# Bias of a residual added from SBUF, rows stored plainly, sums in two passes, nine warm-up matmuls

## The chip, the cores and the metric

The kernel runs on one core of one Trainium2 chip. The metric is device microseconds of one execution, and of several runs the median counts. A profiled execution gives, beside its own device time, the span from its first to its last instruction.

## The reference

The reference is a decoder trunk of two layers on 1024 tokens of 1024 channels, in float32. Layer 0 mixes tokens with a causal Conformer convolution of 31 taps, layer 1 with sliding-window attention. What matters here is what both layers do around the mixer's output `y`:

```python
x = layer_norm(DEEPNORM_ALPHA * x + y, mix_ln_g[i], mix_ln_b[i])
x = layer_norm(DEEPNORM_ALPHA * x + sq_relu_mlp(x, mlp_w_up[i], mlp_w_down[i]),
               mlp_ln_g[i], mlp_ln_b[i])
x = x + (p[i] @ ple_w_proj[i]) * jax.nn.sigmoid(x @ ple_w_gate[i])
```

The normed `x` of the first line is used twice in the second: as input of the MLP, and, times ALPHA, as the residual that is added to the MLP's output. With `xhat` for the normed rows before gain and bias, this residual is ALPHA * g * xhat + ALPHA * b, with `g = mix_ln_g[i]` and `b = mix_ln_b[i]`. The second term is the same for every token; it is the bias of which the title speaks.

## The kernel before

**How the program is made.** The code records all instructions with their reads and writes (`Recorder`, L224) and then orders them by a planner (`schedule`, L343): it plays the program on estimated durations (`cost`) and landing times (`LANDING`, L100), takes on each engine the ready instruction with the lowest priority number, and so fixes the order of every engine's queue and of the DMA queue of SP. `with nc.later(n)` moves the priority of what it encloses n places back, and `with nc.after(op)` lets the planner start it only when `op` has ended in its own play; on the chip only the data and the order of the queues bind. So a change in one place can move instructions elsewhere. All instructions are issued from one helper line (L493 in the profile), so groups are told by their tiles.

**Precision.** Each operand of a product is split into a high and a low part (`split`, L578: ACT casts the high one, DVE subtracts to get the low one), and each product is three matmuls. Weights come by SP into `raw` and are split into `wh` and `wl`, five buffers of each. Large products use Winograd's seven half-size products for eight, for which sums and differences of operands are made on DVE.

**The start (`conv`).** `warm_up` (L843) issues WARM = 7 matmuls on zeros while the first inputs load. Then, in 40 steps, come the input product of the convolution by blocks of 128 channels (`conv_in`, later `conv_seven`), the taps as matmuls on shifted copies (`taps`), whose weights go through `bo`, `E` and `B` buffers, and the stores of intermediate results. At step BIASED = 3 the two layers' bias rows are loaded into the `bo` buffers, multiplied by ALPHA on POOL, and written as one row each to DRAM (`bias0`, `bias1`); in the eight steps after that, `bias_rows` (L746) fills the 1024 rows of the DRAM tensor `mid` of layer 0 with that row, two DMAs of 256 KB (from DRAM to DRAM, on SP's queue) for each of eight tiles of 128 tokens. The same is done for layer 1 in the last down group of layer 0.

**From the convolution to the MLP.** `conv_ln` (L1103) norms the convolution's result in two halves of tokens, each of eight channel blocks. The result is read back from DRAM (`reload`): the first half into X buffers, the second into A buffers. The second half's reads are planned after block SECOND = 4 of the first half, and the reads of the input rows x (into B buffers, four tiles of tokens) after block XB = 3. `mix_out` multiplies by the output weights. `mix_norm` (L707) makes `xhat` for a tile of tokens; its last tiles call `column_forms` (L755), which turns pairs of tiles into channel-major form on PE, applies gain and bias on ACT, and splits the result into the operands of the MLP. Of the four pairs, the first two are kept as they are; with the last two, token sums for Winograd's products T[1] to T[4] are made on DVE, each split as soon as it is there, channel block by channel block. T[4] lives in B buffers.

**The residual.** `keep_row` (L738) multiplies xhat by ALPHA * g in place and adds it to `mid` by an accumulating DMA on POOL's queue: at once for the rows in B buffers, and one by one during the up product for those in A (`late_rows`). Thirty-two such DMAs of 256 KB run in all, sixteen for each layer.

**The down product.** It goes in three groups of chunks, DOWN = (0, 1, 2), (3, 4), (5, 6, 7) (`down_seven`, L1569). A group runs seven products, each of 24 matmuls for every chunk, and adds each to one or two quarters of x in SBUF (`add_to`); operands are made in eight blocks of `xTh` and `xTl`, two for each chunk of a product. In the first group (`begin`), `residual` (L1631) adds `mid` to x: sixteen accumulating DMAs on POOL's queue, four after the second, fifth, sixth and seventh product. The middle group also prepares gate weights (`gate_plain`). The last group norms the rows (`layer_norm`), and `ple_seven` adds the gated embedding.

Of the kernel before, what the change touches and what calls it, by code (L numbers as in the profile page):

```python
# [10 lines left out]
F32 = mybir.dt.float32  # L11
F32R = mybir.dt.float32r
AF = mybir.ActivationFunctionType
ALU = mybir.AluOpType
AXIS = mybir.AxisListType.X

P = 128
T = 1024
D = 1024
KB = D // P  # L20
NT = T // P
HT = 512
# [5 lines left out]
ALPHA = 4.0 ** 0.25  # L28
# [18 lines left out]
BEHIND = 200  # L47
ROWS_BY = 0
BIAS_BY = 200
BIASED = 3  # L50
XB, SECOND = 3, 4
FIRST_OUT = "shifted", 6, 1, 1
PLAIN = 2
ZC = 288
# [19 lines left out]
XHAT = ['av'] * 8  # L74
ROWS_LATE = 400, 400, 400, 400
COLUMN_SLACK = 1500
RAWS = "raw", "zz", "raw", "raw"
MIX = (0, ((0, 1, 4, 5),)), (1, ((0, 1), (4, 5), (2, 3), (6, 7))), (0, ((2, 3), (6, 7)))
TAIL = (0, (2,)), (1, (0, 2)), (0, (3,)), (1, (1, 3))
# [2 lines left out]
DOWN = (0, 1, 2), (3, 4), (5, 6, 7)  # L82
SUMMED = (0, 7)
GRAIN = 64
WARM = 7
EARLY = 2
URGENT = 200
PLAN = (
# [439 lines left out]
class Emit:  # L528
# [209 lines left out]
    def keep_row(self, i, t, q, g):  # L738

        nc = self.nc  # L740
        v = self.x[t][q]
        cols = slice(q * HT, (q + 1) * HT)
        nc.vector.scalar_tensor_tensor(out=v, in0=v, scalar=ALPHA, in1=g, op0=ALU.mult, op1=ALU.mult)
        nc.gpsimd.dma_start(self.mid[i][t][:, cols], v, accum_op=ALU.add)

    def bias_rows(self, i, tiles=range(NT)):  # L746

        for t in tiles:
            for q in range(2):
                cols = slice(q * HT, (q + 1) * HT)  # L750
                at = np.broadcast_to(np.arange(cols.start, cols.stop), (P, HT))
                src = View(self.bias[i].buf, at, P, (("fn", lambda a, cols=cols: a[:, cols].to_broadcast([P, HT])),))
                self.nc.sync.dma_start(self.mid[i][t][:, cols], src)

    def column_forms(self, i, p):  # L755

        nc = self.nc
        tt, sub = nc.vector.tensor_tensor, ALU.subtract
        if p == 0:
            self.cols = {}  # L760
            self.T = {}
        for k in range(4):
            ps = self.ps("tr")
            nc.slack = COLUMN_SLACK
            for q in range(2):
                for j in range(2):
                    o = q * 256 + j * P
                    nc.tensor.transpose(ps[:, o : o + P], self.x[2 * p + j][q][:, k * P : (k + 1) * P], self.ident)
            nc.slack = 0.0
            v = self.column_home(k, p) if p < 2 else self.sb("z")  # L770
            for q in range(2):
                kb = k + 4 * q
                c = slice(q * 256, (q + 1) * 256)
                gc, bc = (self.mixc[:, 16 * i + 8 * m + kb : 16 * i + 8 * m + kb + 1] for m in range(2))
                nc.scalar.activation(v[:, c], ps[:, c], AF.Identity, bias=bc, scale=gc)
            at = slice(p * 256, (p + 1) * 256)
            if p < 2:
                self.cols[k, p] = v
                w = v.rearrange("p (q t) -> p q t", q=2)
                self.split(w, *[x[:, k : k + 5 : 4, at] for x in (self.xTh, self.xTl)])  # L780
                continue
            r = self.cols[k, p - 2]
            L, R = slice(0, 256), slice(256, HT)
            to = slice(p % 2 * 256, (p % 2 + 1) * 256)
            T = {n: [x[:, to] for x in self.token_home(n, k)] for n in range(1, 5)}
            s = self.sb("z")[:, L]
            tt(out=v[:, L], in0=v[:, L], in1=r[:, L], op=sub)
            tt(out=s, in0=v[:, R], in1=v[:, L], op=sub)
            self.split(s, *T[2])
            tt(out=r[:, L], in0=s, in1=r[:, L], op=sub)  # L790
            self.split(r[:, L], *T[3])
            self.split(v[:, L], *T[1])
            self.split(v[:, R], *[x[:, k + 4, at] for x in (self.xTh, self.xTl)])
            tt(out=r[:, R], in0=r[:, R], in1=s, op=sub)
            self.split(r[:, R], *T[4])

    def column_home(self, k, p):

# [44 lines left out]
    def warm_up(self):  # L843
# [4 lines left out]
        ps = self.ps()  # L848
        for k in range(WARM):
            nc.tensor.matmul(ps, z[:, 0:P], z, start=True, stop=True)  # L850
# [29 lines left out]
    def conv(self):  # L880

        nc, d, ws = self.nc, self.d, self.ws
# [188 lines left out]
        def reload(c, e):  # L1071

            Z[c, e] = self.sb("XA"[e])
            src = View(zd[c].buf, np.arange(T), P, (("fn", lambda a: a[:, e * HT : (e + 1) * HT]),))
            nc.sync.dma_start(Z[c, e], src)
# [54 lines left out]
        last = None  # L1130
        zd = [nc.tile(f"zd{c}", (P, T), F32, "DRAM") for c in range(8)]
# [6 lines left out]
        for n in range(32 + LAG):  # L1138
            next(ins, None)
            if n == ready:  # L1140
                for k in range(4):
                    self.differences(k)
            if n in (ready, ready + 1):
                for j in ((3, 2), (4, 1))[n - ready]:
                    for k in range(4):
                        self.split_form(j, k)
            if n == BIASED:
                for i in range(2):
                    for q, v in enumerate(self.load_row("bo", d["mix_b"][i : i + 1])):
                        nc.gpsimd.tensor_scalar(out=v, in0=v, scalar1=ALPHA, scalar2=0.0, op0=ALU.mult, op1=ALU.add)  # L1150
                        nc.sync.dma_start(self.bias[i][:, q * HT : (q + 1) * HT], v[0:1])
            if BIASED < n <= BIASED + NT:
                self.bias_rows(0, (n - BIASED - 1,))
            if n >= LAG:
                next(outs, None)
            if n == BACK[0]:
                for c in range(BACK[1]):
                    reload(c, 0)
            if n == 30 + LAG:
                last = nc.ops[-1]  # L1160
            if n >= 32 + LAG - 8 // EARLY * EMBEDDED:
                with nc.later(EMBED_BY):
                    for k in range(min(EARLY, 8 * EMBEDDED - HELD - made)):
                        next(early)
                        made += 1
# [4 lines left out]
        with nc.after(marks["shifted", 7, 1, 1]):  # L1170
            bo = self.load_row("bo", d["b_out"])
# [11 lines left out]
        r = conv_stats()  # L1183
# [58 lines left out]
    def mix_out(self, i, w, g, gate):  # L1242
# [3 lines left out]
        for n, (cc, groups) in enumerate(MIX):  # L1246
            g_ = gate[n > 0]
            ws.add(*[lambda ap=w[cc, u], tag=RAWS[u], g_=g_: self.prep(ap, gate=g_, tag=tag) for u in range(4)])
        for cc, groups in MIX:
# [319 lines left out]
    def down_seven(self, i, cs, begin, end):  # L1569

        nc, d = self.nc, self.d
# [36 lines left out]
        def product(ops, to, bank=None, last=False):  # L1608
            new = bank is None
            bank = [self.ps() for t in range(4)] if new else bank  # L1610
            if last and to == [(0, 1)]:
                for k in range(3):
                    nc.move("ps", "tr")
            every = [(k, t) for k in range(len(ops)) for t in range(4)]
            for k, t in sorted(every, key=lambda x: x[::-1]) if last else every:
                self.part(bank[t], *ops[k], t, new and k == 0, k == len(ops) - 1, not new)
            for t in range(4):
                for h, q in to:
                    self.add_to(t + 4 * h, q, bank[t])
            with nc.after(nc.ops[-1]):  # L1620
                for k in range(0 if begin or end else min(2, len(plain))):
                    self.gate_plain(i, *plain.pop(0))
            for t in range(4 if last and not i else 0):
                with nc.after(bank[t]):
                    self.bias_rows(1, (t + 4 * to[0][0],))
            for t in range(4 if last else 0):
                with nc.later(LATE + NORM_STEP * t if to == [(0, 1)] else 0):
                    self.layer_norm(t + 4 * to[0][0], gb)
            return bank

        def residual(h, q):  # L1631
            for t in range(4 * h, 4 * h + 4) if begin else ():
                nc.gpsimd.dma_start(self.x[t][q], self.mid[i][t][:, q * HT : (q + 1) * HT], accum_op=ALU.add)

        def each(f, own=False):
            return [formed(*f(c), own) for c in order]
# [281 lines left out]
    def attention(self):  # L1918
# [95 lines left out]
        for cc, n in TAIL[1:]:  # L2014
            ws.add(*[lambda ap=d["w_o"][cc, u], tag=RAWS[u]: self.prep(ap, tag=tag) for u in range(4)])
        for k, (cc, pairs) in enumerate(TAIL):
# [94 lines left out]
    def program(self):  # L2111
        nc = self.nc
# [12 lines left out]
        for i in range(2):  # L2125
            for t in range(NT):
                nc.slots(f"mid{i}_{t}", [f"mid{i}_{t}"])
            for c in range(NC):
                for k in range(8):
                    nc.slots(f"hid{i}_{c}_{k}", [f"hid{i}_{c}_{k}"])  # L2130
        for k in ("qd", "kd", "ad", "bias0", "bias1", *[f"zd{c}" for c in range(8)]):
            nc.slots(k, [k])
        self.bias = [nc.tile(f"bias{i}", (1, D), F32, "DRAM") for i in range(2)]
        self.qd = nc.tile("qd", (NH * P, T), F32, "DRAM")
        self.kd = nc.tile("kd", (4 * P, 2 * T), F32, "DRAM")
        self.ad = nc.tile("ad", (P, 4 * T), F32, "DRAM")
# [141 lines left out]
```

## Time and profile before

| | us |
|---|---|
| median of three runs | 2102.75 (2100.43 to 2102.86) |
| profiled execution | 2099.18 |
| its span | 2097.5 |
| PE busy in it | 2078.6 |
| DVE, ACT, POOL busy | 1598.6, 1145.6, 205.5 |

The profile's page gives busy times, the chain of work that ended last, and groups of instructions. A timeline row is start, length, engine, line, operation, output<-inputs, shapes and count, and in brackets the idle time of the engine before it with what ended it. A row of the windows view has, for a stretch, the busy time of PE, PE's weight loads, DVE, ACT and POOL with their numbers of instructions, then the granted clock of PE, the share of the 16 DMA engines in use, and GB/s. In the waits view a row is who waited for whom: us in total, times, longest. Matmuls overlap, so the time that one takes of PE is the distance between starts, not its length. Stages by time: convolution to 290, output product and preparation of the MLP to 400, up product of layer 0 to 670, down product to 960, gate and embedding to 1100, attention to 1340, then layer 1 in the same order.

### The profile page before, as it was taken

What the parts mean: (1) busy time and instruction counts of PE and PEld (TensorE: products, weight loads), DVE (VectorE), ACT (ScalarE), POOL (GpSimd) and SP (SyncE); (2) the same over time, 40 slices, a digit from 0 to 9 for tenths busy, and PEclk for the clock granted to TensorE, in tenths of its full rate; (3) what the DMA queues carried; (4) which work ended last, traced back from release to release, by engine and by line L of the source; (5) the groups of instructions that cost most, each with busy time, mean ns of one, the idle gap of its engine ahead of it and who ended that gap; (6) DMA issues with size and microseconds to landing.
All of it is one profiled execution on the core that took longest, in us unless ns stands there. A gap on an engine that the chain in (4) does not pass through costs nothing.

```text
span 2097.5 us, 28728 instructions
## 1 busy us (share of the span) xinstructions
PE 2078.6 (99%) x9863; PEld 1731.5 (83%) x9863; DVE 1598.6 (76%) x2502; ACT 1145.6 (55%) x2086; POOL 205.5 (10%) x365
## 2 busy tenths in 40 slices
PE   9999999999999999999999999999999999999998
PEld 7888878888888888888889878878888888888887
DVE  7777798877775768779774798886777656788796
ACT  6566765755555544424433798675555555344343
POOL 0000001000000010000000576110000000100000
PEclk9999999999999999999999999999999999999999
DMA  8878955488868878555777672556888697885526
GB/s 254 264 218 244 323 186 134 145 250 273 266 235 289 253 202 279 186 181 141 244 217 219 214 238 85 141 171 192 255 257 274 205 328 220 222 284 169 163 75 197
DMA packets 232858, 455.70 MB, mean 217 GB/s; under 512 B 22148, under 2 KB 79748, under 8 KB 232712
## 3 DMA queue, kind: packets, MB, share of 16 engines
q1 hardware_dynamic: 223352, 436.83, 63.7%
q0 software_dynamic: 9216, 16.78, 5.1%
q8 instruction: 77, 1.26, 0.3%
q14 instruction: 69, 0.57, 0.1%
q10 hardware_dynamic: 144, 0.26, 0.1%
HBM read 313.27 MB, written 148.91 MB: 220 GB/s over the span
## 4 chain that ended last, share of the span: by engine, by line
PE 88%; DVE 6%; DMA 2%; ACT 2%; issue 1%; POOL 1%; SPq 0%; DVEq 0%; ACTq 0%; POOLq 0%
PE ps L493 67%; PE tr L493 20%; DVE wl L493 1%; DVE A L493 1%; DMA mid<-bias 1%; DVE B L493 1%; ACT z L493 1%; DVE xTl L493 1%; DVE sm L493 1%; DMA raw<-in_w_in_dram 1%; DMA mid<-B 1%; DVE X L493 0%; DVE z L493 0%; ACT t L493 0%; POOL sm L493 0%
## 5 line engine op out<-in xcount | busy, mean ns | idle before, releaser
L493 PE MATMUL ps<-xTh,wh 128*128 128x512 f32 (+1 forms) x672 | 261.9, 391 | 1.2 <-ACT xTh L493 1.2
L493 PE MATMUL ps<-xTl,wh 128*128 128x512 f32 (+1 forms) x672 | 262.4, 391 | 0.2 <-DVE xTl L493 0.2
L493 PE MATMUL ps<-xTh,wl 128*128 128x512 f32 (+1 forms) x672 | 261.8, 390 | 0.3 <-DVE wl L493 0.3
L493 DVE TENSOR_TENSOR wl<-raw,wh 128x1024 fp32r<-128x1024 f32 (+2 forms) x146 | 153.1, 1049 | 101.3 <-ACT wh L493 100.9
L493 PE MATMUL ps<-xTh 128*128 128x512 f32 x552 | 214.7, 389 | 0.0
L493 PE MATMUL ps<-xTl,xTh 128*128 128x512 f32 x552 | 214.7, 389 | 0.0
L493 PE MATMUL ps<-xTh,xTl 128*128 128x512 f32 x552 | 214.7, 389 | 0.0
L493 ACT CAST wh<-raw 128x1024 fp32r<-128x1024 f32 (+2 forms) x146 | 132.0, 906 | 98.4 <-PE ps L493 67.2
L493 ACT CAST wh<-g 128x512 fp32r<-128x512 f32 x152 | 90.0, 620 | 154.5 <-PE ps L493 59.3
L493 ACT CAST xTh<-wh 128x1024 fp32r<-128x1024 f32 x84 | 88.3, 1051 | 152.9 <-PE ps L493 119.1
L493 DVE TENSOR_TENSOR wl<-g,wh 128x512 fp32r<-128x512 f32 x152 | 101.5, 686 | 64.0 <-ACT wh L493 63.3
L493 PE MATMUL ps<-wl,xTh 128*128 128x512 f32 (+1 forms) x400 | 150.1, 376 | 0.0
L493 PE MATMUL ps<-wh,xTh 128*128 128x512 f32 (+1 forms) x400 | 150.0, 376 | 0.0
L493 PE MATMUL ps<-wh,xTl 128*128 128x512 f32 (+1 forms) x400 | 149.4, 375 | 0.2 <-DVE xTl L493 0.2
L493 PEld LDWEIGHTS ps<-xTh,wh 128*128 128x128 f32 x672 | 126.5, 189 | 27.7 <-ACT xTh L493 1.9
L493 PEld LDWEIGHTS ps<-xTh,wl 128*128 128x128 f32 x672 | 126.7, 189 | 26.1 <-DVE wl L493 0.7
L493 PEld LDWEIGHTS ps<-xTl,wh 128*128 128x128 f32 x672 | 126.9, 189 | 24.9 <-DVE xTl L493 0.9
L493 DVE TENSOR_TENSOR xTl<-wh,xTh 128x1024 fp32r<-128x1024 f32 x84 | 102.6, 1221 | 56.8 <-ACT xTh L493 56.6
L493 PEld LDWEIGHTS ps<-xTl,xTh 128*128 128x128 f32 x552 | 103.6, 188 | 21.7
L493 PEld LDWEIGHTS ps<-xTh 128*128 128x128 f32 x552 | 103.6, 188 | 21.5
L493 PEld LDWEIGHTS ps<-xTh,xTl 128*128 128x128 f32 x552 | 103.6, 188 | 21.3
L493 DVE TENSOR_TENSOR xTl<-wl,xTh 128x1024 fp32r<-128x1024 f32 x76 | 92.4, 1218 | 1.7 <-ACT xTh L493 1.7
(398 smaller groups left out, 5056.1 us busy)
## 6 DMA issues: line engine op xcount, KB each, us to landing
wh<-hid SPq DMA_DIRECT2D x84, 512.0 KB, 4.5
raw<-in_w_up_dram SPq DMA_DIRECT2D x67, 512.0 KB, 4.7
wl<-in_w_down_dram SPq DMA_DIRECT2D x58, 512.0 KB, 4.7
hid<-t SPq DMA_DIRECT2D x92, 256.0 KB, 3.6
hid<-zz SPq DMA_DIRECT2D x68, 256.0 KB, 4.3
raw<-hid SPq DMA_DIRECT2D x26, 512.0 KB, 4.2
mid<-bias SPq DMA_DIRECT2D x32, 256.0 KB, 6.8
z<-scr SPq DMA_DIRECT2D x32, 256.0 KB, 4.7
```

Of the source, the lines that this page charges most:

```text
L493: getattr(getattr(nc, o.eng), o.name)(*a, **k)
```

## The change

- `warm_up` issues nine matmuls on zeros for seven.
- The gates of `conv`'s end: x rows after block 1 of the first half (XB), the second half's reads after block 6 (SECOND).
- `bias_rows`, its 32 fills, the DRAM rows and the step that made them are gone.
- `keep_row` stores its row plainly on SP's queue.
- In the middle down group the bias row is loaded into the two `bo` buffers and multiplied by ALPHA on POOL, and `residual` adds it to x by accumulating DMAs from SBUF on POOL's queue, at the same places of the group as in the first one.
- `column_forms` makes the sums of a channel block first; the splits of T[3], T[1], the plain quarter and T[4] get priorities 40, 60, 60 and 60 places later (FORMED), so that they come in a second pass.

```diff
-BIASED = 3
-XB, SECOND = 3, 4
+XB, SECOND = 1, 6
+FORMED = 40, 60, 60, 60
-WARM = 7
+WARM = 9
 def keep_row(self, i, t, q, g):
     ...
     nc.vector.scalar_tensor_tensor(out=v, in0=v, scalar=ALPHA, in1=g, op0=ALU.mult, op1=ALU.mult)
-    nc.gpsimd.dma_start(self.mid[i][t][:, cols], v, accum_op=ALU.add)
-
-def bias_rows(self, i, tiles=range(NT)):
-    ...
+    nc.sync.dma_start(self.mid[i][t][:, cols], v)
 def column_forms(self, i, p):
     ...
     self.split(s, *T[2])
     tt(out=r[:, L], in0=s, in1=r[:, L], op=sub)
-    self.split(r[:, L], *T[3])
-    self.split(v[:, L], *T[1])
-    self.split(v[:, R], *[x[:, k + 4, at] for x in (self.xTh, self.xTl)])
     tt(out=r[:, R], in0=r[:, R], in1=s, op=sub)
-    self.split(r[:, R], *T[4])
+    for n, (a, to) in enumerate((
+        (r[:, L], T[3]), (v[:, L], T[1]), (v[:, R], [x[:, k + 4, at] for x in (self.xTh, self.xTl)]), (r[:, R], T[4])
+    )):
+        with nc.later(FORMED[n]):
+            self.split(a, *to)
 def conv(self):
     ...
-            if n == BIASED:
-                for i in range(2):
-                    for q, v in enumerate(self.load_row("bo", d["mix_b"][i : i + 1])):
-                        nc.gpsimd.tensor_scalar(out=v, in0=v, scalar1=ALPHA, scalar2=0.0, op0=ALU.mult, op1=ALU.add)
-                        nc.sync.dma_start(self.bias[i][:, q * HT : (q + 1) * HT], v[0:1])
-            if BIASED < n <= BIASED + NT:
-                self.bias_rows(0, (n - BIASED - 1,))
 def down_seven(self, i, cs, begin, end):
     ...
-            for t in range(4 if last and not i else 0):
-                with nc.after(bank[t]):
-                    self.bias_rows(1, (t + 4 * to[0][0],))
+        if not begin and not end:
+            bias = self.load_row("bo", d["mix_b"][i : i + 1])
+            for v in bias:
+                nc.gpsimd.tensor_scalar(out=v, in0=v, scalar1=ALPHA, scalar2=0.0, op0=ALU.mult, op1=ALU.add)
+
         def residual(h, q):
-            for t in range(4 * h, 4 * h + 4) if begin else ():
-                nc.gpsimd.dma_start(self.x[t][q], self.mid[i][t][:, q * HT : (q + 1) * HT], accum_op=ALU.add)
+            for t in range(4 * h, 4 * h + 4) if not end else ():
+                src = self.mid[i][t][:, q * HT : (q + 1) * HT] if begin else bias[q]
+                nc.gpsimd.dma_start(self.x[t][q], src, accum_op=ALU.add)
```

More of the change, by code (lines that the diff above doesn't have):

```diff
@@ L743, in keep_row @@
         nc.vector.scalar_tensor_tensor(out=v, in0=v, scalar=ALPHA, in1=g, op0=ALU.mult, op1=ALU.mult)
-        nc.gpsimd.dma_start(self.mid[i][t][:, cols], v, accum_op=ALU.add)
-    def bias_rows(self, i, tiles=range(NT)):
[L748 to L753, printed above, removed]
+        nc.sync.dma_start(self.mid[i][t][:, cols], v)
     def column_forms(self, i, p):
@@ L2130, in program @@
                     nc.slots(f"hid{i}_{c}_{k}", [f"hid{i}_{c}_{k}"])
-        for k in ("qd", "kd", "ad", "bias0", "bias1", *[f"zd{c}" for c in range(8)]):
+        for k in ("qd", "kd", "ad", *[f"zd{c}" for c in range(8)]):
             nc.slots(k, [k])
-        self.bias = [nc.tile(f"bias{i}", (1, D), F32, "DRAM") for i in range(2)]
         self.qd = nc.tile("qd", (NH * P, T), F32, "DRAM")
```

## The prediction

> **What bounds the kernel now.** I read the page first, then windows of the span, then the matmuls that waited, then the chain back from those waits. The page says that TensorE is the bound nearly throughout:
>
> ```profile
> span 2097.5 us, 28728 instructions
> PE 2078.6 (99%) x9863; PEld 1731.5 (83%) x9863; DVE 1598.6 (76%) x2502; ACT 1145.6 (55%) x2086; POOL 205.5 (10%) x365
> ```
>
> The change removes no matmul and adds two, so nothing can be won except in the 18.9 us in which PE is idle and where its clock is low. The timeline of PE alone shows where; the bracket is idle time before the row and who ended it. The rows without a bracket are there for the spacing of matmuls.
>
> ```profile
> 1.51 3.35 PE L493 MATMUL ps<-t 128*128 128x512 f32 x7 [1.51 <-DVE t L493]
> 6.02 1.22 PE L493 MATMUL ps<-xTh,wh 128*128 128x512 f32 x2 [1.15 <-ACT xTh L493]
> 9.60 0.63 PE L493 MATMUL ps<-xTh,wl 128*128 128x512 f32 x1
> 10.03 0.63 PE L493 MATMUL ps<-xTh,wh 128*128 128x512 f32 x1
> 10.46 0.44 PE L493 MATMUL ps<-xTl,wh 128*128 128x512 f32 x1
> 11.43 0.40 PE L493 MATMUL ps<-xTh,wl 128*128 128x512 f32 x1
> 11.66 0.39 PE L493 MATMUL ps<-xTh,wh 128*128 128x512 f32 x1
> ...
> 65.68 2.29 PE L493 MATMUL ps<-z,E 128*128 128x256 f32 x9 [3.98 <-DVE E L493]
> 290.90 0.50 PE L493 MATMUL tr<-wh,xTh 128*128 128x512 f32 x1 [1.79 <-ACT wh L493]
> 292.59 0.50 PE L493 MATMUL tr<-wl,xTh 128*128 128x512 f32 x1 [0.72 <-DVE wl L493]
> 362.57 0.87 PE L493 MATMUL ps<-ident,A 128*128 128x128 f32 x6 [0.72 <-ACT A L493]
> 367.79 0.39 PE L493 MATMUL ps<-xTl,wh 128*128 128x256 f32 x1 [0.24 <-DVE xTl L493]
> 1389.09 0.66 PE L493 MATMUL tr<-ident,A 128*128 128x128 f32 x4 [0.91 <-ACT z L493]
> 1402.89 0.50 PE L493 MATMUL ps<-xTh,wl 128*128 128x512 f32 x1 [0.26 <-DVE wl L493]
> 1542.64 0.73 PE L493 MATMUL ps<-E,wh 128*128 128x512 f32 x2 [0.89 <-ACT t L493]
> ```
>
> Four places lie where the change works: the start, the stall at 65.68 (the largest), the hand-over from the convolution to its output product at 289 to 293, and in each layer the preparation of the MLP (361 to 368 and 1388 to 1403). Followed back, the stall at 65.68 and the two preparations pass through the rows that this change rewrites (start, length, what):
>
> ```profile
> 36.46 6.51 DMA mid<-bias
> ...
> 43.85 10.19 DMA mid<-bias
> ...
> 54.13 7.88 DMA raw<-in_w_in_dram
> ...
> 354.83 5.12 DMA mid<-B
> ...
> 1382.38 5.53 DMA mid<-B
> ```
>
> A weight load is issued at 54.13 because a bias fill that took 10.19 us has just landed, and its cast and the tap weights behind it come too late for PE.
>
> **The change, part by part.** The sum is made on the profiled execution: 2099.18 us, span 2097.47 and 1.71 around it. The median of the three runs shown, 2102.75, is 3.57 above it; no row explains that, so I carry it over unchanged.
>
> *Two more warm-up matmuls.* In the cold state matmuls start 0.43 us apart (9.60 to 10.03), later 0.23 (11.43 to 11.66). Eleven real ones, from 6.02 to 10.46, start cold, which loses 11 x 0.20 = 2.2 us. Seven warm-ups end at 4.86 and leave a hole of 1.15; two more fill 0.86 of it and end near 5.72, before the data at 6.02, so they delay nothing. The gain is at least 0 (the clock does not care) and at most 2.2. A partial fit is likelier than either end; how long a cold phase lasts when it is fresh is seen at the stall:
>
> ```profile
> 64.00:66.00 2.00, 0.32 (x1) 0.32 (x2) 2.00 (x4) 2.00 (x4) 0.00 (x0) 0.79 0.98 333
> 66.00:68.00 2.00, 2.00 (x10) 2.00 (x10) 2.00 (x4) 0.08 (x1) 0.00 (x0) 0.50 0.77 237
> 68.00:70.00 2.00, 2.00 (x9) 1.57 (x9) 2.00 (x5) 1.77 (x3) 0.11 (x1) 0.86 0.61 157
> ```
>
> The third column from the end is the granted clock: (0.42 + 1.00 + 0.28) / 0.5 = 3.4 us at half clock. If the start's cold phase ends one such period sooner, at 7.1, 1.7 us are won; I take 1.5, since nothing shows that casts keep up with a fast PE before 10.46. [...]
>
> *No bias fills in the convolution.* Sixteen DRAM-to-DRAM fills of 256 KB, four loads and four POOL multiplications go from the first 55 us. What they cost the SP queue, how busy the DMA engines are there, and what a transfer costs (the queues' packets, MB and share of 16 engines; then issues with KB and us to landing):
>
> ```profile
> SPq L493 <- DMA mid<-bias: 9.6, 11, 1.9
> ```
>
> ```profile
> 25.00:66.00 41.00, 37.02 (x167) 30.52 (x167) 32.45 (x49) 21.72 (x36) 3.06 (x2) 0.99 0.90 248
> ```
>
> ```profile
> q1 hardware_dynamic: 223352, 436.83, 63.7%
> q0 software_dynamic: 9216, 16.78, 5.1%
> ...
> hid<-z SPq DMA_DIRECT2D x32, 256.0 KB, 3.8
> ...
> mid<-B POOLq DMA_DIRECT2D x16, 256.0 KB, 5.7
> ...
> B<-mid POOLq DMA_DIRECT2D x16, 256.0 KB, 6.7
> ```
>
> The first row is SP's own waits between 9 and 70 us: 9.6 us of it behind fills. By q1, 256 KB cost 0.637 x 2097.5 / 436.83 x 0.262 = 0.80 us of all sixteen engines, so sixteen fills are 12.8 of the 36.9 us for which the engines are busy between 25 and 66 (0.90 of 41, the second row's last column but one). PE needs its operand 3.98 us sooner, 5.5 with the warm-up's gain; the queue alone gives 9.6. With the idle time goes the cold phase it set off: from 65.68 on 0.16 + 1.00 + 0.28 = 1.4 us of lost clock. Bounds 0 (another load of the same crowded stretch is late instead) and -5.4; I take -4.7, nearest the row of SP's waits, and leave 0.7 for the next late load, the tap weights.
>
> *The reloads at the convolution's end (XB, SECOND).* The rows of x come two blocks sooner in the order, and the second half of the convolution's result two blocks later, so the last weights of the output product need no longer queue behind it:
>
> ```profile
> 273.91 4.71 SPq L493 DMA_DIRECT2D A<-zd  x8
> 279.03 0.99 SPq L493 DMA_DIRECT2D raw<-in_w_out_dram  x2
> ```
>
> ```profile
> 288.44 0.82 ACT L493 ACTIVATE A<-A,cst 128x512 f32<-128x512 f32 x1 [4.53 <-DVE A L493]
> ...
> 289.81 1.04 ACT L493 CAST wh<-raw 128x1024 fp32r<-128x1024 f32 x1
> ```
>
> ACT, in order, holds the weight cast that PE wants behind the second half's activation, idle 4.53 us before it. If the cast goes first, both waits (1.79 + 0.72 = 2.51) go; if the second half slips by the 4.71 us that its eight issues take, and PE meets it, that much is lost. Between -2.5 and +4.7 I take -1.2: the order that removes the wait is what the new gates ask for, but DVE has this work to do anyway.
>
> *Rows stored plainly, sums in two passes (FORMED).* Thirty-two accumulating stores move from POOL's queue to SP's and become plain. SP's queue loses 32 fills and gets 32 stores, so its issue work stays equal; POOL loses 32 issues, which stood among its reciprocal roots for the norm. A plain store of this size lands in 3.8 us, these in 5.12 and 5.53 on the chain, and the B buffers that wait for them are those of the last operand of the product. On SP what queues behind a store whose row DVE has not made yet is the next weight load; the five weight buffers cover that. The waits at stake are 0.72 + 0.24 + 0.91 + 0.26 = 2.13. DVE is the next late there:
>
> ```profile
> 1350.00:1400.00 50.00, 49.09 (x235) 40.53 (x234) 44.94 (x110) 39.03 (x87) 8.03 (x9) 1.00 0.59 170
> ```
>
> The third pair is DVE, 44.94 of 50 us, ACT 39.03. Splits pushed back by 40 or 60 places only change the order of equal work, so a loss of the same 2.1 is the other bound. I take -1.3.
>
> *Bias added in the middle down group.* Per layer: two row loads, two POOL multiplications, sixteen accumulating DMAs from SBUF into x on POOL's queue. By q0 one costs 0.051 x 2097.5 / 64 = 1.67 us of all engines, 26.7 us per layer. The groups (span, PE, PEld, DVE, ACT, POOL, clock, DMA share, GB/s):
>
> ```profile
> 785.00:865.00 80.00, 80.00 (x355) 66.24 (x354) 65.92 (x83) 36.45 (x45) 2.65 (x3) 1.00 0.79 256
> 1815.00:1895.00 80.00, 80.00 (x355) 66.24 (x354) 65.99 (x84) 35.73 (x45) 3.51 (x4) 1.00 0.79 258
> ```
>
> ```profile
> ACT xTh L493 <- PE ps L493: 34.1, 12, 3.5
> ```
>
> 63.2 + 26.7 = 89.9 us of DMA work in 80, though four of the sixteen are issued after the group's last product. The cover: ACT's casts wait 34.1 us in the first of these groups for PE to free an operand block, not for loads; there are eight blocks, a product of one chunk takes two and 24 matmuls x 80 / 355 = 5.4 us, so operands are made up to 16 us ahead, and the weight loads further. I take 0; without that cover it costs 9.9 us per layer. The next add into the rows accumulated last comes with the third product of the last group, two products of 72 matmuls or 32 us later, against 6.7 us to land. The sixteen fills of layer 1's rows that go from the last group of layer 0 save nothing: PE is never idle there.
>
> Sum: -1.5 - 4.7 - 1.2 - 1.3 + 0 = -8.7. 2099.18 becomes 2090.5; the median 2102.75 becomes 2094.
>
> **The rivals.** (a) *The early stall only moves.* For it: the DMA engines are 0.98 busy from 64 to 66, ten us after that weight load went out. Then the 4.7 stays: 2098.7. [...] (c) *The second half of the convolution comes late*: instead of -1.2 the hand-over costs +4.7, 2099.9. It decides from the point where the eight reads land later than PE's second round of output products; against it, their first activation ran at 288.44, 9.8 us after the last of them was issued (273.91 + 4.71). (d) The other side, *DMA saturation in the middle group*: where the cover of 16 us is used up, the overflow of 9.9 us per layer shows as PE idle, 2094 + 19.8 = 2113.8, slower. Against it: accumulating DMAs in the first group (B<-mid, 6.7 us to land) run with PE never idle. [...]
>
> **How the numbers follow.** A change below 0.2%, 4.2 us, can hardly be told from none. The forecast gets 0.62 (own range 2089 to 2098), (a) 0.15, (b) 0.12, (c) 0.07, (d) 0.04. Faster, below 2098.5: nearly all of the forecast and (b), half of (a), little of (c): 0.82. Same 0.13, slower 0.05. The range goes from 2088 (all of the 2.2, 5.4, 2.5 and 2.1 and some more) to 2101, which takes in (a), (b) and (c) and leaves out (d).
>
> **What would show it.** Right: no PE wait over 1 us between 55 and 75 and the granted clock 1.00 there; the half-rate spacing at the start ends before 9 us; the waits at 290.90 and 292.59 below 1 us in sum; those of the MLP's preparation halved; PE busy throughout the two middle groups. It would be wrong if a wait on tap weights stands where the old one stood, or if a new order of the queues opens waits where there is none now, in the up products or the attention, which the sum holds at 0. The wait at 1542.64 should stay.

## The result, and the profile after

| | before | after |
|---|---|---|
| median, us | 2102.16 (2100.43 to 2102.86, 4 runs) | 2084.9 (2084.39 to 2086.02, 4 runs) |
| profiled execution, us | 2099.18 | 2084.83 |
| its span, us | 2097.5 | 2083.1 |

The ratio is 0.992, 95% interval 0.9903 to 0.9937: faster, by 17.3 us in the medians and by 14.35 from profile to profile, where the prediction had 8.7. The measured 2084.9 lies below its range, which began at 2088. PE, idle for 18.9 us before, is idle for 8.7 now (the head of the page and its busy engines):

```profile
span 2083.1 us, 28780 instructions
PE 2074.4 (100%) x9865; PEld 1731.9 (83%) x9865; DVE 1596.7 (77%) x2502; ACT 1144.9 (55%) x2086; POOL 203.4 (10%) x365
```

PE's own timeline after: the start, and the only two waits for data above 0.35 us that are left behind it.

```profile
1.51 4.21 PE L493 MATMUL ps<-t 128*128 128x512 f32 x9 [1.51 <-DVE t L493]
...
6.80 0.60 PE L493 MATMUL ps<-xTh,wl 128*128 128x512 f32 x1
7.23 0.41 PE L493 MATMUL ps<-xTl,wh 128*128 128x512 f32 x1
7.47 0.39 PE L493 MATMUL ps<-xTh,wl 128*128 128x512 f32 x1
...
376.91 0.73 PE L493 MATMUL ps<-E,wh 128*128 128x512 f32 x2 [0.52 <-ACT t L493]
...
500.00 0.73 PE L493 MATMUL ps<-E,wh 128*128 128x512 f32 x2 [0.38 <-ACT t L493]
```

The stall of 3.98 at 65.68 is gone, the waits of 1.79 and 0.72 at the hand-over are gone, those of the MLP's preparation too, and also the 0.89 at 1542.64, which was to stay. Matmuls are 0.43 us apart up to 7.23 and 0.24 after it; before, up to 10.46. Four stretches of the windows view (columns as in the prediction: PE, PEld, DVE, ACT, POOL, granted clock, DMA share, GB/s): the convolution's first part with the place of the old stall, layer 1's preparation, and the two middle down groups:

```profile
25.00:66.00 41.00, 41.00 (x199) 34.69 (x198) 38.03 (x60) 24.06 (x41) 0.22 (x2) 1.00 0.60 177
1350.00:1400.00 50.00, 49.88 (x237) 41.14 (x236) 43.72 (x97) 39.49 (x80) 4.45 (x4) 1.00 0.49 171
785.00:865.00 80.00, 80.00 (x355) 66.27 (x354) 61.63 (x76) 36.35 (x45) 13.97 (x16) 1.00 0.97 298
1810.00:1890.00 80.00, 80.00 (x354) 66.29 (x354) 63.36 (x78) 35.54 (x44) 13.94 (x16) 1.00 0.98 299
```

With the fills gone the DMA engines are 0.60 busy between 25 and 66, against 0.90. The middle groups are now full of transfers, 0.97 and 0.98 against 0.79, and PE does not notice (80.00 busy of 80).

Idle rows miss what a low clock costs: the stall of 3.98 in the first profile lost 5.65 with the half clock behind it (0.50 from 65.14 to 68.55). So for the kernels below the distance from each matmul's start to the next was summed beyond the distance of undisturbed ones (0.227 us for 512 columns, 0.120 for 256, 0.109 to 0.112 for 128). Lost time of PE in us, each kernel from its one profiled execution; "again" is the same kernel in a later profile:

| kernel | start | early stall, 25 to 80 | hand-over, 240 to 310 | MLP prep. 0 | 420 to 660 | MLP prep. 1 | 1430 to 1660 |
|---|---|---|---|---|---|---|---|
| before | 5.18 | 5.65 | 3.28 | 2.53 | .06 | 2.35 | 1.35 |
| before again (b_again) | 3.26 | 7.18 | 4.29 | 2.92 | .85 | 2.67 | 1.10 |
| b_warm9 | 2.82 | 6.02 | 6.09 | 2.14 | .07 | 2.40 | .83 |
| b_xb16 | 2.96 | 5.90 | .20 | 3.32 | .75 | 2.29 | 1.11 |
| b_formed | 3.18 | 5.58 | 3.31 | 5.73 | .64 | 2.45 | .71 |
| a_bias_only | 2.94 | .13 | 4.92 | 1.79 | .12 | 1.61 | .21 |
| a_fills | 2.83 | 4.56 | .20 | 1.29 | .04 | 1.18 | 0 |
| a_fills_act | 2.52 | 5.99 | .39 | 1.29 | .04 | .28 | 0 |
| a_xb34 | 2.51 | .13 | 4.92 | .79 | .05 | 1.61 | .16 |
| a_split1 | 3.03 | .13 | .19 | 3.59 | .05 | 1.62 | .04 |
| a_warm7 | 3.50 | .13 | .19 | 1.24 | .04 | .24 | .18 |
| a_pool_again | 2.80 | .13 | .20 | 1.02 | 0 | .25 | 0 |
| a_twice | 2.46 | .13 | .21 | 1.25 | .02 | .34 | 0 |
| after | 2.86 | .13 | .19 | 1.27 | .73 | .60 | 0 |
| after again | 2.88 | .13 | .19 | 1.26 | .05 | .25 | .07 |

From the row "before" to the row "after" the seven places lose 14.6 us together, which accounts for the 14.35 between the two profiles.

### The profile page after: what moved, and what is told of

It is laid out like the page before. It is cut to its first block, busy times and chain, and to the rows that moved or that the text cites. A ratio compares the mean times of both kernels' runs of the same rounds, so it can differ in the third digit from the quotient of the medians.

```text
span 2083.1 us, 28780 instructions
## 1 busy us (share of the span) xinstructions
PE 2074.4 (100%) x9865; PEld 1731.9 (83%) x9865; DVE 1596.7 (77%) x2502; ACT 1144.9 (55%) x2086; POOL 203.4 (10%) x365
## 3 DMA queue, kind: packets, MB, share of 16 engines
q8 instruction: 77, 1.26, 0.3%
## 4 chain that ended last, share of the span: by engine, by line
PE 95%; ACT 2%; DVE 1%; DMA 1%; issue 0%; POOL 0%; SPq 0%; DVEq 0%; ACTq 0%
PE ps L493 74%; PE tr L493 21%; ACT z L493 1%; DMA t<-proj 1%; DMA raw<-in_w_up_dram 0%; ACT wh L493 0%; DVE t L493 0%; DVE wl L493 0%; ACT t L493 0%; DVE z L493 0%; ACT xTh L493 0%; POOL z L493 0%; DMA raw<-gsum 0%; DVE xTl L493 0%; DVE A L493 0%
## 5 line engine op out<-in xcount | busy, mean ns | idle before, releaser
L493 PE MATMUL ps<-xTh,wh 128*128 128x512 f32 (+1 forms) x656 | 254.6, 390 | 0.0
L493 PE MATMUL ps<-xTl,wh 128*128 128x512 f32 (+1 forms) x656 | 254.4, 389 | 0.0
L493 PE MATMUL ps<-xTh,wl 128*128 128x512 f32 (+1 forms) x656 | 254.2, 388 | 0.0
L493 PE MATMUL ps<-wh,xTh 128*128 128x512 f32 (+1 forms) x360 | 135.6, 377 | 0.0
L493 PE MATMUL ps<-wh,xTl 128*128 128x512 f32 (+1 forms) x360 | 135.4, 377 | 0.1
L493 PE MATMUL ps<-wl,xTh 128*128 128x512 f32 (+1 forms) x360 | 135.2, 376 | 0.0
```

The lines of the kernel that those rows point to most:

```text
L493: getattr(getattr(nc, o.eng), o.name)(*a, **k)
```

## The experiments

Kernels named a_ are the kernel after with something undone or added, those named b_ the kernel before with one part done. Times are medians; each ratio is to the kernel before, run beside it, with its 95% interval. Beside these kernels, before had medians of 2098.98 to 2099.89 and the kernel after, run again, 2083.86, so that the gain is nearer to 15 us in these runs than to 17.3.

**Where do the 3.57 us between the profile and the median come from?** The two kernels once more, unchanged.

> The kernel before, unchanged, profiled once more: the earlier profile (2099.2 us) lies 3 us under the median of its timed runs. Theory 'spread': the extra time is in the start and in the stall near 65 us, whose cold phases (and DMA landings) differ from execution to execution; then this profile has the same order of waits, with the PE stall near 65 us between 3 and 7 us, all other PE waits within 0.3 us of the first profile, and its time follows that stall. Rival 'offset': timed executions are simply 3 us longer than profiled ones; then the stall is 4.0 us again, and the timed runs still give 2101 to 2103.

Measured: 2100.81 (2095.9 to 2103.42, 12 runs), ratio 1.0001 (0.9991 to 1.0011); its profile 2101.29. Before scatters over some 8 us or more (2094.89 to 2104.2 in 23 runs of it beside these kernels). Its two largest waits stand where they stood in the first profile, 4.69 us for 3.98 and 1.81 for 1.79. What they cost differs by more: 7.18 for 5.65 and 4.29 for 3.28 in the table. The two waits, and at the hand-over two windows of 3.41 us each, as long as the half-clock stretch behind the stall of the first profile (65.14 to 68.55), here called a clock period:

```profile
PE ps L493 <- DVE E L493: 4.7, 1, 4.7
PE tr L493 <- ACT wh L493: 1.8, 1, 1.8
```

```profile
287.57:290.98 3.41, 1.60 (x8) 1.02 (x7) 3.41 (x7) 2.89 (x4) 0.00 (x0) 1.00 0.01 5
290.98:294.40 3.42, 3.02 (x8) 1.91 (x7) 3.42 (x5) 2.76 (x5) 0.00 (x0) 0.50 0.35 75
```

The wait of 1.8 us is followed by 3.4 us at half clock. In the profile on which the prediction was made, with periods counted on from 65.14 by estimate, the same waits are shared out over two of them, and the granted clock stays at 1.00:

```profile
287.01:290.42 3.41, 2.10 (x10) 1.41 (x8) 3.41 (x7) 1.95 (x3) 0.00 (x0) 1.00 0.02 10
290.42:293.84 3.42, 2.22 (x8) 1.53 (x9) 3.42 (x6) 2.79 (x5) 0.00 (x0) 1.00 0.04 12
293.84:297.25 3.41, 3.41 (x16) 2.81 (x15) 3.41 (x6) 1.92 (x3) 0.00 (x0) 1.00 0.58 221
```

> The changed kernel, unchanged, on the same chip as the three beside it. Theory 'windows': the 3 us that separated the profile of before from its timed runs were half-clock windows set off by its waits; the changed kernel has no wait long enough, so its runs lie within 3 us of each other, 2083 to 2086, and those of before scatter by 8 us or more. Rival 'offset': timed runs lie 3 us over the profiled one here too.

Measured: 2083.86 (2083.6 to 2083.97, 4 runs), ratio 0.9926 (0.9912 to 0.9939), profile 2083.95. The kernel after has little scatter and no distance between profile and median, so the 3.57 was no constant of the measurement.

What was it? Two things on record bear on that. First, the 2102.75 was the median of three runs. The 76 later runs of the kernel before, all taken together, have a median of 2099.71 (2094.89 to 2106.13), 0.53 above the first profile. So most of the 3.57 is where three runs lay in this scatter; why they lay high isn't settled. Second, the mean granted clock of each of the 76 is known. The sixteen runs at 0.999 have a median of 2098.04 us, the seventeen at 0.996 one of 2101.47, so the lower clock goes with the longer time. It is not the whole scatter: the sixteen at 0.999 alone lie between 2095.85 and 2100.05. The eight runs of the kernel after have 0.999 or 1.0.

**The early stall: the fills, and if so, by SP's queue or by the DMA engines?** First the bias alone moved:

```diff
 kernel after, with
-XB, SECOND = 1, 6
+XB, SECOND = 3, 4
-WARM = 9
+WARM = 7
 column_forms: every split where its sum is made (no FORMED)
```

> Only the bias is moved (no fills, plain rows, accumulation in the middle down group); seven warm-ups, the reload gates and the split order are as before. Theory 'four places': the stall near 65 us goes (5.5 us with its cold phase) and part of the MLP preparation's waits (1 to 2 us), the waits at the convolution's end (2.5 us) and the start stay: 2092 to 2096. Rival 'fills are all': without the fills everything behind them is in time as well, and this gives nearly the whole change: 2086 to 2088.

Measured: 2090.12 (2088.9 to 2090.53), ratio 0.9949 (0.9937 to 0.9961), between the two ranges that were expected. More than half of the gain is this part: the early stall goes (.13), the loss between 1430 and 1660 falls to .21, and both preparations lose less (1.79 and 1.61) with the rows stored plainly. Then the kernel after with layer 0's fills put back, into DRAM rows that nothing reads:

```diff
 kernel after, with bias_rows, its step in conv, and layer 0's 16 fills
+                self.nc.sync.dma_start(self.fill[t][:, cols], src)
```

> The changed kernel with the sixteen fills of layer 0 (and the four loads, POOL multiplications and row stores that make them) put back into the convolution's first steps, written to DRAM rows that nothing reads. Theory 'four places': a PE stall near 60 us comes back, worth 4 to 6 us with its cold phase, and nothing else: 2089 to 2091. Rival 'early stall only moves': the DMA engines were not what mattered and the time stays at 2085 to 2086.

Measured: 2090.5 (2089.06 to 2093.41), ratio 0.9955 (0.9942 to 0.9968), 5.6 to 6.6 us above the kernel after. So the fills cause the stall. It is back at its old place, and the window from 25 to 66 looks as before:

```profile
62.36 1.61 PE L494 MATMUL ps<-z,E 128*128 128x256 f32 x9 [2.56 <-DVE E L494]
```

```profile
25.00:66.00 41.00, 38.44 (x173) 31.80 (x172) 34.25 (x53) 22.47 (x38) 3.44 (x3) 0.97 0.91 266
```

The chain back from it runs, as in the kernel before, through a fill for which SP's queue waits before it issues a weight load:

```profile
41.62 10.32 DMA mid<-bias
...
52.03 6.58 DMA raw<-in_w_in_dram
```

The same with the fills issued by ACT (`self.nc.scalar.dma_start`), so that SP's queue holds none of them:

> The changed kernel with layer 0's sixteen fills put back as before, but issued on ACT's queue instead of SP's; nothing reads them. Theory 'queue': the early stall came from weight loads standing in SP's order behind issues that waited for fills to land; with the fills in another queue the stall near 62 us is gone or under 1 us: 2084 to 2086. Rival 'bandwidth': the fills keep the DMA engines 0.9 busy whoever issues them, loads land late and the stall stays at 2 to 3 us idle with its half-clock window: 2088 to 2091.

Measured: 2089.53 (2087.38 to 2091.74), ratio 0.9957 (0.9945 to 0.997). The stall stays, and is larger:

```profile
59.05 3.89 PE L494 MATMUL ps<-z,E 128*128 128x256 f32 x18 [3.87 <-issue]
```

```profile
25.00:66.00 41.00, 37.13 (x166) 31.05 (x165) 33.26 (x51) 21.16 (x36) 4.32 (x3) 0.96 0.92 272
```

Its loads of tap weights and, in the second fence, those of the kernel after (KB, us from issue to landing):

```profile
bo<-in_w_dw_dram SPq DMA_DIRECT2D x4, 288.0 KB, 6.6
```

```profile
bo<-in_w_dw_dram SPq DMA_DIRECT2D x3, 288.0 KB, 4.2
```

The tap weights that PE waits for land in 6.6 us instead of 4.2 although the fills stand in another queue. The time is the one that 'bandwidth' expected. But this does not show that the DMA engines alone make the stall. In a_fills, with the fills in SP's own queue, the tap weights landed in 3.9 us and PE stalled all the same. And here the fills stand in the queue of ACT, whose casts PE needs: the last part of the chain back from the stall has ACT issuing a fill (ACTq), then its casts, then 1.56 us in which PE waited for nothing that the profile shows:

```profile
53.72 1.61 ACTq L494
55.38 1.04 ACT wh L494
...
57.49 1.56 issue
```

So the experiment took the fills out of SP's queue, but put them into that of another engine on PE's path. The fills stall PE from either queue; how much of that is the order of a queue and how much the 16 engines, 0.91 to 0.92 busy in these two runs, stays open.

**The hand-over's gates.** Undone in the kernel after, and done alone in the kernel before:

```diff
 a_xb34 (kernel after)          b_xb16 (kernel before)
-XB, SECOND = 1, 6             -XB, SECOND = 3, 4
+XB, SECOND = 3, 4             +XB, SECOND = 1, 6
```

> The changed kernel with the old reload gates (3, 4). Theory 'hand-over': PE's two waits near 290 us (1.8 and 0.7 us) return and in most executions take a half-clock window of 3.4 us or two with them (1.7 us each): 2088 to 2091. Rival 'queue was late': the waits at the hand-over came from work that was late since the early stall; with that gone the old gates do as well: 2085 to 2086.

Measured: 2088.44 (2086.19 to 2090.07), ratio 0.9948 (0.9936 to 0.996), 3.5 to 4.6 us above the kernel after, although the waits that return are 2.5 in sum. The rest is the clock (the window of PE's waits, then again one clock period a row):

```profile
PE tr L493 <- ACT wh L493: 1.8, 1, 1.8
PE tr L493 <- DVE wl L493: 0.7, 1, 0.7
```

```profile
281.98:285.40 3.42, 1.60 (x6) 1.04 (x7) 3.42 (x6) 3.33 (x5) 0.00 (x0) 1.00 0.00 0
285.40:288.81 3.41, 3.41 (x10) 2.64 (x9) 3.41 (x6) 1.44 (x2) 0.00 (x0) 0.50 0.57 185
```

> The kernel before with the new reload gates alone. Theory 'hand-over': the waits near 290 us and the half-clock windows that they set off go, the early stall stays: 4 us less than before, 2095 to 2097, and less scatter. Rival 'queue was late': with the early stall still there the weights come late anyway, under 1.5 us less than before.

Measured: 2096.28 (2095.16 to 2099.62, 11 runs) beside 2098.98, ratio 0.9989 (0.998 to 0.9998): 2.7 us by this part alone, and the hand-over's loss is .20. It works as predicted: ACT casts the weights, at the right time, ahead of the second half's activation (kernel after):

```profile
270.20 2.06 SPq L493 DMA_DIRECT2D raw<-in_w_out_dram  x2
272.31 5.89 SPq L493 DMA_DIRECT2D A<-zd  x8
```

```profile
277.94 1.05 ACT L493 CAST wh<-raw 128x1024 fp32r<-128x1024 f32 x1 [0.28 <-DMA raw<-in_w_out_dram]
...
283.22 0.82 ACT L493 ACTIVATE A<-A,cst 128x512 f32<-128x512 f32 x1 [4.23 <-DVE A L493]
```

**The two passes, and the rows.** One pass in the kernel after (the lines of `column_forms` as before), and the two passes alone in the kernel before.

> The changed kernel with each token sum split as soon as it is there (one pass). Theory 'rows matter': the waits in the MLP's preparation went with the plain stores, and one pass costs under 1 us: 2084.5 to 2086. Rival 'passes matter': the waits at 360 and 1390 us come back, 1.5 to 2 us in sum, perhaps with a half-clock window: 2086.5 to 2089.

Measured: 2088.27 (2086.84 to 2088.35), ratio 0.9945 (0.9933 to 0.9958), 3.4 to 4.4 us above the kernel after. The waits are where the passes were (PE's waits between 255 and 420, then layer 1's largest in the timeline). Of the first, the kernel after has 0.52 too, at 376.91; the other two it has not:

```profile
PE ps L493 <- ACT X L493: 1.2, 1, 1.2
PE tr L493 <- ACT xTh L493: 0.5, 1, 0.5
```

```profile
1379.73 0.66 PE L493 MATMUL tr<-ident,A 128*128 128x128 f32 x4 [1.00 <-ACT z L493]
```

> The kernel before with the two-pass split alone (accumulating row stores kept). Theory 'passes': undoing the passes in the changed kernel cost 2.3 us near 360 and 1.0 near 1390, so they give 2 to 3 us here: 2096 to 2098 where before has 2099 to 2100. Rival 'rows first': with accumulating stores the B buffers come late anyway, and the passes alone give under 1 us.

Measured: 2097.99 (2094.24 to 2100.65, 11 runs), ratio 0.9992 (0.9983 to 1.0001): alone, the passes bring nothing that can be told, though the interval reaches from a loss of 0.2 us to a gain of 3.6. There DVE's next work waits for an accumulating store, as the chain to PE's wait shows:

```profile
352.67 7.80 DMA mid<-B
...
360.91 1.22 DVE wl L494
...
363.10 1.00 PE ps L494 x6
```

The store took 7.80 us here, and PE waited 3.36 before 363.10; behind it, until 367.4, matmuls of 256 columns start 0.21 us apart, and 0.12 after that; with this slow stretch the loss is 5.73 (table). So in this execution a late store took what the passes could give. That they pay only where the rows are stored plainly fits, but is not shown: the interval also allows most of what they gave on plain rows. Does it matter by which queue? The plain stores on POOL's queue, twice:

```diff
-        nc.sync.dma_start(self.mid[i][t][:, cols], v)
+        nc.gpsimd.dma_start(self.mid[i][t][:, cols], v)
```

> The changed kernel with the rows' plain stores issued on POOL's queue instead of SP's. Theory 'plain': what helped was that a plain store lands sooner than an accumulating one; the time stays at 2085 to 2086. Rival 'queue': POOL's issues stand again among the roots of the norm and delay them: waits of 0.5 to 1.5 us return near 360 and 1390: 2085.5 to 2087.5.

> The changed kernel with the rows' plain stores on POOL's queue, beside the changed kernel itself. Theory 'same': the queue that stores plain rows makes no difference, within 0.8 us of the changed kernel. Rival 'SP queue': the stores stand in SP's order before weight loads, and without them the small waits of the up product go: 1 to 2 us faster than the changed kernel.

Measured: 2083.18 (2082.93 to 2084.48), ratio 0.9924 (0.9912 to 0.9937), and 2083.55 (2083.37 to 2084.66), ratio 0.9926 (0.9912 to 0.9939): as the kernel after. The landing of the stores, on SP's queue (kernel after) and on POOL's (a_pool_again):

```profile
mid<-B SPq DMA_DIRECT2D x16, 256.0 KB, 2.8
```

```profile
mid<-B POOLq DMA_DIRECT2D x16, 256.0 KB, 2.7
```

Before, accumulating on POOL's queue, 5.7. The queue is not what made them slow, then; the accumulation is what is left.

**The warm-up.** WARM = 7 in the kernel after, WARM = 9 in the kernel before.

> The changed kernel with seven warm-ups. [...] Rival 'always late': the half-rate phase ends near 10.5 us in each execution: 2086.7 to 2087.3, without scatter.

> The kernel before with nine warm-ups. Theory 'clock window': the half-rate spacing ends before 8 us rather than at 10.5, but PE then only arrives sooner at the stall near 65 us, whose end is set by DMA: the stall grows by what the start wins, and the time stays within 1 us of before. Rival 'additive': the start's 2 us are kept: 2099.5 to 2100.5.

Measured: 2084.43 (2083.27 to 2085.29), ratio 0.9928 (0.9916 to 0.9939), and 2098.99 (2096.09 to 2103.61, 11 runs), ratio 0.9992 (0.9984 to 1.0001): nothing that the times can tell, either way. In the table's column "start" the six kernels with seven warm-ups lost 2.94 to 5.18 us, the nine with nine 2.46 to 3.03; their middles, 3.2 and 2.8, are 0.4 apart. The first profile of before, with 5.18 and a slow start until 10.46, is the odd one out; the same kernel again is fast from 7.71:

```profile
7.71 0.39 PE L493 MATMUL ps<-xTh,wh 128*128 128x512 f32 x1
7.94 0.40 PE L493 MATMUL ps<-xTl,wh 128*128 128x512 f32 x1
```

**The cover of the middle groups.** Half the bias, added twice, so 32 accumulating DMAs per layer in place of 16:

```diff
-                nc.gpsimd.dma_start(self.x[t][q], src, accum_op=ALU.add)
+                for k in range(1 if begin else 2):
+                    nc.gpsimd.dma_start(self.x[t][q], src, accum_op=ALU.add)
```

> The changed kernel with half of the bias added twice in the middle down group, so 32 accumulating DMAs per layer there instead of 16. The DMA engines are already 1.0 busy in that group, and 16 more are some 24 us of all engines per layer. Theory 'cover': operands are made two or three products ahead and the third group needs half of the DMA time, so the backlog is worked off with PE idle under 2 us per layer: 2084 to 2088. Rival 'saturation': PE waits for weights by the backlog less the cover of 16 us, 8 us or more per layer: above 2100.

Measured: 2085.56 (2084.0 to 2086.84), ratio 0.9933 (0.9921 to 0.9945), against 0.9926 (0.9912 to 0.9939) for the kernel after: 1.7 us more, with overlapping intervals. Its middle group, and the landing of operands and weights in it:

```profile
780.00:860.00 80.00, 80.00 (x355) 66.26 (x354) 63.47 (x78) 35.71 (x45) 17.43 (x20) 1.00 1.01 303
```

```profile
wh<-hid SPq DMA_DIRECT2D x11, 512.0 KB, 10.3
wl<-in_w_down_dram SPq DMA_DIRECT2D x8, 512.0 KB, 9.3
```

The same in the kernel after, and in the kernel before:

```profile
wh<-hid SPq DMA_DIRECT2D x11, 512.0 KB, 6.3
wl<-in_w_down_dram SPq DMA_DIRECT2D x9, 512.0 KB, 7.2
```

```profile
wh<-hid SPq DMA_DIRECT2D x11, 512.0 KB, 4.9
wl<-in_w_down_dram SPq DMA_DIRECT2D x9, 512.0 KB, 4.3
```

The engines are full, landings double, and PE stays at 80.00 of 80: the cover is larger than even this needs. The 1.7 us of the medians aren't seen in this profile (span 2082.3) and stay open.

## Why the prediction was right in its direction and too small

| term | in the sum | first profiles, before to after | medians of the runs that undo it, or do it alone |
|---|---|---|---|
| warm-up | -1.5 | -2.3 | none that can be told (a_warm7, b_warm9) |
| fills gone | -4.7 | -5.5 | -5.6 to -6.6 (a_fills) |
| hand-over | -1.2 | -3.1 | -3.5 to -4.6 (a_xb34), -2.7 (b_xb16) |
| plain rows and passes | -1.3 | -3.0 | -3.4 to -4.4 for the passes (a_split1) |
| middle groups | 0 | 0 | 0 |
| layers' up products | 0 | -0.7 | not separated |
| profile to median | 0 | -3.5 (3.57 to 0.07) | 76 later runs of before: 0.53 above its first profile |

Between the forecast of 2094 and the measured 2084.9 lie 9.1 us. The terms of the sum were 8.7 together where the table has 14.6, which makes 5.9 of it; the carried distance makes about the rest.

*The largest single step that failed* is "no row explains that, so I carry it over unchanged". The kernel after has 0.07 in place of the 3.57. The median of three scattering runs was taken for the time of the kernel; 76 runs put it at 2099.71. A part of the scatter is the clock: the first profile of before had one period at half clock between its start and PE's last matmul, at the stall of 65.68 (0.50 from 65.14 to 68.55); b_again had two there (some 6.8 us at half clock by estimate, from the 0.79, 0.50, 0.50 and 0.72 granted in 60 to 64, 64 to 66, 66 to 68 and 68 to 70) and one more at the hand-over (0.50 from 290.98 to 294.40), and the time of the 76 runs rises as their clock falls. The first profile of the kernel after has 1.00 from 8 to its last matmul; in both of its profiles no place behind the start lost more than 1.27 us, less than the 1.7 that a period at half clock costs by estimate (half of 3.41). The kernel scatters by 2.4 us. How much of the 3.57 was clock and how much the choice of three runs stays open.

*The hand-over* failed in its size: -1.2 was taken between -2.5 and +4.7 because DVE "has this work to do anyway". PE never met it. The upper bound was mis-set too: 2.5 counted idle time alone, without the half-clock periods, by estimate worth 1.7 us each, of which one followed on such a wait of 1.8 us in b_again and in a_xb34. Measured, the term is -2.7 to -4.6. Rival (c) falls: the second half's first activation runs at 283.22. That is 5.2 us sooner than before, while PE came there 7.8 us sooner (2.3 and 5.5 in the table), so against PE it slipped by some 2.6, and PE did not wait for it.

*The MLP's preparation* failed in its size as well: 2.13 of idle rows stood against 4.88 us of lost spacing in the table (2.53 and 2.35), so the bound was too low from the start; measured, the loss fell by 3.0. "DVE is the next late there" was wrong for PE: with DVE 43.72 busy of 50, hardly less than the 44.94 before, PE rose from 49.09 to 49.88. "Splits pushed back only change the order of equal work" missed that the order is what PE waits for (a_split1).

*The early stall* was right in its cause, the fills (a_fills), and near in size; no later load took its place, so the 0.7 held back was not needed and rival (a) falls, with PE at 41.00 of 41. The reason given, SP's 9.6 us behind fills, is what the chains of before and a_fills show, but it isn't the only way: with the fills out of SP's queue the stall was as large (a_fills_act).

*The warm-up* was wrong by 1.1 (1.5 in the sum, 0.4 between the middles of the column "start"): the slow start of one profile was read as what seven warm-ups do. With seven, the start lost from 2.94 to 5.18 in six profiles, and from 3.26 to 5.18 in the two of the kernel before alone.

*The middle groups* were right, cover and all; rival (d) falls. POOL's DMAs landed in 8.8 us beside DVE busy 61.63 of 80, with PE busy 80.00 (issues in the first middle group of the kernel after):

```profile
A<-bo POOLq DMA_DIRECT2D x8, 256.0 KB, 8.8
```

That is 2.1 us more than the 6.7 of the first group's adds before, and far from the 32 that stood behind the last ones. Where the 2.1 come from, no run here shows.

*The up products*, held at 0, won the wait of 0.89 at 1542.64 that was to stay. The loss between 1430 and 1660 is small in every kernel with the bias moved (.21 at most) and .71 to 1.35 in every kernel without, so it belongs to that part; by which step isn't settled. A wait of 0.38 at 500.00 came in one profile of the kernel after and not in the other.

No kernel here is clearly faster than the kernel after; a_pool_rows is its equal.

## What to carry to other kernels

Where PE is the bound, price its waits by the distances between matmul starts, not by idle rows: behind a wait of 1.8 us the granted clock was 0.50 for 3.41 us in b_again and a_xb34, by estimate 1.7 us more. When executions scatter, three runs and one profile don't say where the kernel lies: here three runs had 2102.75 and 76 had 2099.71. So look at the granted clock of each run, and take more of them, before a distance between profile and median is carried over. Work that is moved to another engine's queue is a test of the first queue only if the second isn't on PE's path too. And of two edits on one stage, try each undone from the whole as well as done alone: the passes brought nothing that could be told on accumulating stores and 3.4 to 4.4 us on plain ones.

## What the runs showed of the hardware that was not expected

- *Behind 3.41 us in which PE was busy 1.60, the granted clock was 0.50* for the next 3.41 (b_again, a_xb34); in the first profile, with 2.10 and 2.22 busy, it stayed at 1.00. The longest gap in these stretches was 1.81 us. In one profile (b_warm9) a second half-clock period followed on one in which PE was busy 2.69:

```profile
286.82:290.23 3.41, 1.62 (x7) 0.77 (x5) 3.41 (x7) 3.27 (x5) 0.00 (x0) 1.00 0.01 4
290.23:293.64 3.41, 2.69 (x7) 2.11 (x7) 3.41 (x5) 2.78 (x4) 0.00 (x0) 0.50 0.37 121
293.64:297.06 3.42, 3.42 (x9) 2.65 (x9) 3.42 (x7) 1.95 (x4) 0.00 (x0) 0.50 0.55 186
```

- *An accumulating store of 256 KB landed in 5.7 us* (rows in B, kernel before), *a plain one in 2.7 to 2.8*, from POOL's queue (a_pool_again) or from SP's (kernel after).
- *Full DMA engines by themselves cost PE nothing* in the middle groups of a_twice (share 1.01, landings doubled to 10.3 us, PE busy 80.00 of 80 in each). Between 25 and 66, with a share of 0.90 to 0.92, PE stalled by 2.56 to 3.98 us; there the chains of before and a_fills run through a fill that SP's queue waits for, so that the share alone stalls PE is not shown.
